# Six instead of four accumulation banks opened together at the start of each SwiGLU of a two-layer hybrid trunk

## The chip, the cores and the metric

The kernel runs on one core of a Trainium2 chip. The metric is the time of one execution on the device in microseconds (us). Three runs of the kernel before were timed, and their median stands for it. One execution was recorded by the hardware profiler, and every row below comes from that one.

Five engines matter here. PE is the matrix engine (its weight loads are shown apart, as PEld), DVE the vector engine, ACT the scalar engine, POOL the general one, and SP issues the transfers from memory. Each engine works through its own queue in order and waits on semaphores for the others.

## The reference, cut to what matters

256 tokens of width 1024 go through two layers. Each layer is a half-step SwiGLU, a mixer (neighbourhood attention beside a long convolution), a second half-step SwiGLU, and a gated per-layer input:

```python
for i in range(DEPTH):
    x = x + 0.5 * swiglu(rmsnorm(x, g_ffa[i]), w_ffa_gate[i], w_ffa_up[i], w_ffa_down[i])
    ...                                   # mixer: x = x + y @ w_out[i]
    x = x + 0.5 * swiglu(rmsnorm(x, g_ffb[i]), w_ffb_gate[i], w_ffb_up[i], w_ffb_down[i])
    x = x + jax.nn.sigmoid(rmsnorm(x, g_ple[i]) @ w_ple_gate[i]) * (p[i] @ w_ple_proj[i])
return rmsnorm(x, g_final)

def swiglu(h, w_gate, w_up, w_down):
    return (jax.nn.silu(h @ w_gate) * (h @ w_up)) @ w_down
```

So there are four SwiGLUs. The inner width is 2816, that is 22 blocks of 128 columns for the gate and 22 for the up product.

## The kernel before, in words

**Layout.** The activations are kept transposed: `x[c]`, c = 0 to 7, is a block of 128 channels by 256 tokens. For a product the block is scaled by the norm's gain and split into two parts, high and low, that lie side by side in one `xg` tile of 128x512: ACT writes the high half (L368), DVE the low half (L370), both in `prep`. The norm's factor 1/rms is not applied to the input. It is found meanwhile (`Rstd`) and multiplied onto the products later (`rb`, L444, used at L489 and L490).

**Weights.** They come as 128x128 tiles in exactly the order in which PE will use them, packed by `_weights` on the host. SP loads 16 tiles at a time (1 MB). Each half of 8 tiles is cast by ACT to a high part `wh` (L285) and DVE (at times POOL) computes the low part `wl` (L288). There are six buffers each for `wh` and `wl` (`WBUFS`), so a cast for a later half waits until PE has used up an earlier one.

**Products.** `Wide.mm` issues one wide matmul (L191: `wh` against high and low of `xg`, 512 columns) and keeps a narrow one (L200: `wl` against the high part, 256 columns) for later. After every eight wides, or when a bank's last block is reached, the kept narrow ones are issued. A gate or up block of 128 columns takes eight wides and eight narrow ones, one of each for every input block c, summed in one of the eight accumulation banks (`psp`, `bufs=8`, each 128x512). When a bank is complete, `taken` frees it: ACT copies its right half to a `gu` tile (L205) and DVE adds the left half (L208).

**The start of a SwiGLU** (`ffn`, L508 to L522). The first four banks (gate and up of the first two column blocks) are filled together: the outer loop runs over the input blocks c, the inner one over the four banks. So PE needs block c only after 4c wides. After that each further bank is filled alone, with all eight input blocks in a row (`product2`). The second loop (`DOWN`) multiplies by the down weights.

**What stands before it.** In the two SwiGLUs that follow the mixer, the eight blocks of the second half of the output projection (`project`, one bank for each block) are multiplied on DVE by the other norm's factor (L944, which reads the bank and thereby frees it), added to `x[c]` (L945), and then scaled and split (L368, L370). In the SwiGLU that follows the gated input, `update` reads the bank at L1043. The very first SwiGLU starts from the loaded input (L1090, L1093), and all banks are free.

**Order.** The side work is written as generators ("fibers"). Every three matmul steps of the main line (`TICK`) all live fibers move one step, the newest first. On PE and ACT the instructions keep this order as written. On the other engines a scheduler puts them in order when the program is built, and it hands out a bank when an older one has been freed. `onward` starts the fiber that turns a finished block into the next `xg` block.

Of the kernel before, what the change touches and what calls it, by code (L numbers as in the profile page):

```python
# [18 lines left out]
P = 128  # L19
# [3 lines left out]
KD = D // P  # L23
DFF = 2816
NF = DFF // P
NH = 8
HY = 512
EPS = 1e-6
HALF = 8
GROUP = 8  # L30

E = mybir.EngineType
# [48 lines left out]
def hybrid_trunk(ctx: ExitStack, tc: tile.TileContext, w, xT, pT, rpb, small, wf, zT, dft, idft, decay, out):  # L81
# [17 lines left out]
    def nm(s):  # L99
        uid[0] += 1  # L100
        return f"{s}{uid[0]}"

    def bank():
        return psp.tile([P, 512], F32, tag="ps", name=nm("ps"))

    def t2(dt=F32, s="t"):
        return k2.tile([P, 512], dt, tag="k2", name=nm(s))

    def t1(dt=F32, s="s"):
        return k1.tile([P, T], dt, tag="k1", name=nm(s))  # L110
# [4 lines left out]
    def f(ap):  # L115
        return ap.bitcast(F32)
# [31 lines left out]
    def spawn(gen, first=False):  # L148
        fb = Fiber(gen)
        Pace.live.insert(0 if first else len(Pace.live), fb)  # L150
        return fb
# [13 lines left out]
    def rest(n):  # L165
        for _ in range(n):
            yield
# [15 lines left out]
    class Wide:  # L183
# [6 lines left out]
        def mm(cls, b, lh, ll, r, start, stop):  # L190
            PE.matmul(b, lh, r, start=start, stop=False)  # L191
            cls.later.append((b[:, T:], ll, r[:, :T], stop))
            if stop or len(cls.later) == GROUP:
                cls.flush()
# [8 lines left out]
    def summed(dst, b):  # L203

        S.copy(dst, b[:, T:])  # L205
        yield
        yield
        V.tensor_add(dst, dst, b[:, :T])  # L208
# [39 lines left out]
    def load():  # L248
# [10 lines left out]
        elif n == 1:  # L259
            for q in range(2):  # L260
                nc.sync.dma_start(x[4 + 2 * q], xT[4 + 2 * q])
                nc.sync.dma_start(raw[:, q * HALF : (q + 1) * HALF], src[:, q * HALF : (q + 1) * HALF])
                nc.sync.dma_start(x[5 + 2 * q], xT[5 + 2 * q])
# [5 lines left out]
    def part(steps=1):  # L269
# [5 lines left out]
        raw = Stream.raws[n // 2]  # L275
        h = whp.tile([P, HALF, P], F32R, tag="wh", name=nm("wh"))
        l = wlp.tile([P, HALF, P], F32R, tag="wl", name=nm("wl"))
        fb = Fiber(None)
        Stream.ready[n] = (h, l, fb)

        def go():
            k = HALF // steps
            for a in range(0, HALF, k):
                src = raw[:, n % 2 * HALF + a : n % 2 * HALF + a + k]
                S.copy(h[:, a : a + k], src)  # L285
                yield
                e = G if Stream.on_pool and n % Stream.on_pool == 0 else V
                e.tensor_sub(l[:, a : a + k], src, f(h[:, a : a + k]))  # L288
            if n % 2:
                Stream.raws.pop(n // 2)  # L290
                load()
# [71 lines left out]
    def new_norm(join=True):  # L363
        Norm.sq = Squares(acc, KD, join)
# [8 lines left out]
    def onward(i, cg, c, before):  # L373

        hl = t2(F32R, "xg")

        def go():
            yield from before
            yield
            yield from prep(i, cg, c, hl)  # L380

        scaled.append((hl, spawn(go())))
# [68 lines left out]
    def norm(xs, at, spread=SPREAD_AT):  # L451
        return Rstd(rb, Norm.sq.parts, D, [fb for _, fb in xs.xs] + early, at, spread)
# [10 lines left out]
    def product2(b, ws, xs):  # L463
        for c in range(KD):
            wh, wl = ws.next()
            Wide.mm(b, wh, wl, xs.both(c), c == 0, c == KD - 1)


    def ffn(i, cg_next, i_next):
        act = []  # L470
        xs = Inputs()
        ws = Tiles()
        rs = norm(xs, STAT_F, SPREAD_F)

        def taken(b):
            dst = t1(s="gu")

            def go():
                yield from rest(EV)
                yield from summed(dst, b)  # L480

            return dst, spawn(go())

        def gated(gate, up, hl):
            (g, gf), (u, uf) = gate, up
            while not (gf.done and uf.done):
                yield
            yield from rs.wait()
            V.tensor_mul(g, g, rb)  # L489
            G.tensor_mul(u, u, rb)  # L490
            yield
            yield
            s = t1()
            S.activation(s, g, AF.Silu)
            yield
            yield
            V.tensor_mul(s, s, u)
            yield
            yield
            S.copy(hl[:, :T], s)  # L500
            yield
            V.tensor_sub(hl[:, T:], s, f(hl[:, :T]))

        def start(gate, up):
            hl = t2(F32R, "act")
            act.append((hl, spawn(gated(gate, up, hl))))

        heads = [bank() for _ in range(4)]  # L508
        for c in range(KD):
            for b in heads:  # L510
                wh, wl = ws.next()
                Wide.mm(b, wh, wl, xs.both(c), c == 0, c == KD - 1)
        heads = [taken(b) for b in heads]
        start(*heads[:2])
        start(*heads[2:])
        for ff in range(2, NF):
            pair = []
            for _ in range(2):
                b = bank()
                product2(b, ws, xs)  # L520
                pair.append(taken(b))
            start(*pair)  # L522
        ws = Tiles()
        new_norm()

        def half_step(c, ps):
            yield from rest(EV)
            for b in (ps[:, :T], ps[:, T:]):
                V.scalar_tensor_tensor(x[c], b, 0.5, x[c], op0=ALU.mult, op1=ALU.add)  # L529

        out = {}
        for c, k in DOWN:
            if k == 0:
                out[c] = bank()
            wh, wl = ws.next()
            hl, fb = act[k]
            fb.finish()
            Wide.mm(out[c], wh, wl, hl, k == 0, k == NF - 1)
            if k == NF - 1:
                onward(i_next, cg_next, c, half_step(c, out.pop(c)))  # L540
# [564 lines left out]
    for i in range(DEPTH):  # L1105
        Stream.on_pool = 0
        flt = spawn(filter_steps(i))
        ffn(i, C_MIX, i)
        flt.finish()
        Stream.on_pool = ON_POOL  # L1110
        mixer(i)
        Stream.on_pool = 0
        given = ple_input(i)
        ffn(i, C_PLE, i)
        ends, outs = ple(i, i == DEPTH - 1, given)
# [47 lines left out]
def _tiles(wm):  # L1163

    k, m = wm.shape
    return wm.reshape(k // P, P, m // P, P).transpose(2, 0, 1, 3)


def _weights(a):
    out = np.empty((DEPTH * PIECES * 16, P, P), np.float32)  # L1170
    at = 0

    def put(t):
        nonlocal at
        t = t.reshape(-1, P, P)
        out[at : at + len(t)] = t
        at += len(t)

    def swiglu(i, s):
        g, u = _tiles(a[f"w_ff{s}_gate"][i]), _tiles(a[f"w_ff{s}_up"][i])  # L1180
        gu = np.stack([g, u], axis=1)
        put(gu[:2].reshape(4, KD, P, P).transpose(1, 0, 2, 3))
        put(gu[2:])
        put(_tiles(a[f"w_ff{s}_down"][i])[tuple(np.array(DOWN).T)])

    for i in range(DEPTH):
        swiglu(i, "a")
        win = _tiles(a["w_in"][i])
        put(win[8:12].transpose(1, 0, 2, 3))
        for kind, j in MIXER:  # L1190
            if kind in "gqx":
                for k in {"g": (20 + j, 16 + j), "q": (j, 4 + j), "x": (12 + 2 * j, 13 + 2 * j)}[kind]:
                    put(win[k])
        wo = _tiles(a["w_out"][i])
        put(wo[:, :4])
        put(wo[:, 4:])
        swiglu(i, "b")
        put(_tiles(a["w_ple_proj"][i]))
        put(_tiles(a["w_ple_gate"][i]))
    assert at == len(out)  # L1200
    return np.ascontiguousarray(out.reshape(-1, 16, P, P).transpose(0, 2, 1, 3)).reshape(-1, P, 16 * P)
# [60 lines left out]
```

## Time and profile before

| | |
|---|---|
| median of 3 runs | 1102.88 us (1100.53 to 1103.08) |
| the profiled execution | 1100.78 us |
| its span, first to last instruction | 1099.0 us |
| PE busy | 1069.0 us, 97% of the span |
| DVE, ACT, POOL busy | 81%, 59%, 28% |
| mean granted TensorE clock | 0.994 |

The span is read against the time of the same execution: 1.78 us lie outside it. A row of a timeline gives the start and the length of a group of instructions of one engine, the line, the operation, the tiles and the count, and in brackets the idle time before it with what ended it. The length of a matmul row runs to the end of its last result, so rows overlap the next ones a little, and the pace is read from start to start. In the four SwiGLUs of this trace the first matmul on an input block stands at 6.2 us, 331.5 us, 550.0 us and 868.2 us.

### The profile page before, as it was taken

How to read it: one execution, taken by the hardware profiler on the slowest of the kernel's cores; microseconds unless marked ns; L12 is line 12 of the kernel's file. 1: busy time of each engine (PE TensorE's matmuls, PEld its weight loads, DVE VectorE, ACT ScalarE, POOL GpSimd, SP SyncE). 2: the span in 40 equal slices, each digit the busy share in tenths (PEclk: the TensorE clock that was granted, in tenths of full speed). 3: DMA queues.
4: the chain of work that ended last, by engine and by line, in shares of the span. 5: the costliest groups of instructions: out<-in, count | busy, mean ns of one | idle time of the engine just before them, and what ended most of it. 6: DMA issues, size and time to landing. Idle time of an engine off the chain costs nothing.

```text
span 1099.0 us, 17994 instructions
## 1 busy us (share of the span) xinstructions
PE 1069.0 (97%) x6716; PEld 964.8 (88%) x6716; DVE 895.5 (81%) x1552; ACT 645.6 (59%) x1182; POOL 306.8 (28%) x270
## 2 busy tenths in 40 slices
PE   7989999999998999999999999999999999999995
PEld 6878888899997888888988888889989888888895
DVE  4999987797999977766789989777899998776665
ACT  6566565377746755544656665544856575554444
POOL 3123231534363311111112113135442721111101
PEclk9999999999999999999999999999999999999998
DMA  8556554554425655555465654554522465555521
GB/s 318 196 201 230 194 189 155 185 185 154 148 78 201 199 189 190 189 192 191 155 208 185 233 192 166 186 185 152 194 77 95 147 207 215 191 193 181 185 94 38
DMA packets 32983, 194.06 MB, mean 177 GB/s; under 512 B 3584, under 2 KB 6528, under 8 KB 10880
## 3 DMA queue, kind: packets, MB, share of 16 engines
q1 hardware_dynamic: 32896, 192.92, 51.1%
q8 instruction: 52, 0.85, 0.3%
q14 instruction: 35, 0.29, 0.1%
HBM read 191.86 MB, written 1.05 MB: 176 GB/s over the span
## 4 chain that ended last, share of the span: by engine, by line
PE 80%; DVE 11%; ACT 4%; issue 3%; DMA 1%; POOL 0%; SPq 0%; DVEq 0%; ACTq 0%; POOLq 0%
PE ps L191 43%; PE ps L200 23%; PE ps L171 4%; PE ps L172 4%; PE ps L170 4%; DVE wl L288 2%; ACT wh L285 1%; DVE rt L399 1%; DVE s L841 1%; DVE x L945 1%; DVE s L944 1%; ACT t L781 1%; DMA t<-in_idft 1%; DVE xg L370 0%; DMA raw<-in_w 0%
## 5 line engine op out<-in xcount | busy, mean ns | idle before, releaser
L288 DVE TENSOR_TENSOR wl<-raw,wh 128x1024 fp32r<-128x1024 f32 (+1 forms) x328 | 416.3, 1272 | 135.1 <-ACT wh L285 113.3
L285 ACT CAST wh<-raw 128x1024 fp32r<-128x1024 f32 (+1 forms) x350 | 362.9, 1042 | 206.0 <-PE ps L191 143.5
L191 PE MATMUL ps<-xg,wh 128*128 128x512 f32 x1408 | 363.2, 396 | 12.3 <-DVE xg L1093 6.6
L191 PEld LDWEIGHTS ps<-xg,wh 128*128 128x128 f32 x1408 | 254.6, 191 | 59.4 <-DVE xg L370 7.5
L200 PEld LDWEIGHTS ps<-xg,wl 128*128 128x128 f32 x1408 | 195.4, 193 | 14.1
L200 PE MATMUL ps<-xg,wl 128*128 128x256 f32 x1408 | 200.5, 284 | 0.0
L490 POOL TENSOR_TENSOR gu<-gu,rb 128x256 f32<-128x256 f32 x88 | 94.8, 1082 | 368.1 <-DVE gu L208 288.0
L191 PE MATMUL ps<-act,wh 128*128 128x512 f32 x704 | 179.0, 392 | 0.0
L356 POOL TENSOR_TENSOR acc<-acc,q 128x256 f32<-128x256 f32 x62 | 68.9, 1112 | 283.7 <-ACT q L353 282.5
L191 PEld LDWEIGHTS ps<-act,wh 128*128 128x128 f32 x704 | 126.3, 189 | 22.1
L170 PE MATMUL ps<-xg,wh 128*128 128x256 f32 x448 | 127.5, 285 | 0.0
L172 PE MATMUL ps<-xg,wl 128*128 128x256 f32 x448 | 126.7, 283 | 0.0
L171 PE MATMUL ps<-xg,wh 128*128 128x256 f32 x448 | 126.7, 283 | 0.0
L200 PEld LDWEIGHTS ps<-act,wl 128*128 128x128 f32 x704 | 97.1, 190 | 7.6
L200 PE MATMUL ps<-act,wl 128*128 128x256 f32 x704 | 99.4, 282 | 0.0
L171 PEld LDWEIGHTS ps<-xg,wh 128*128 128x128 f32 x448 | 85.9, 192 | 0.1
L170 PEld LDWEIGHTS ps<-xg,wh 128*128 128x128 f32 x448 | 85.9, 192 | 0.1
L172 PEld LDWEIGHTS ps<-xg,wl 128*128 128x128 f32 x448 | 85.9, 192 | 0.0
L288 POOL TENSOR_TENSOR wl<-raw,wh 128x1024 fp32r<-128x1024 f32 x22 | 55.9, 2540 | 63.7 <-ACT wh L285 50.9
L208 DVE TENSOR_TENSOR gu<-gu,ps 128x256 f32<-128x256 f32 x176 | 71.9, 412 | 0.1
L205 ACT COPY gu<-ps 128x256 f32<-128x256 f32 x176 | 63.6, 369 | 0.0
L368 ACT ACTIVATE xg<-x,sm 128x256 fp32r<-128x256 f32 x56 | 28.1, 507 | 59.5 <-DVE x L529 40.2
(196 smaller groups left out, 1369.5 us busy)
## 6 DMA issues: line engine op xcount, KB each, us to landing
raw<-in_w SPq DMA_DIRECT2D x172, 1024.0 KB, 4.9
bias<-in_rpb SPq DMA_DIRECT2D x16, 256.0 KB, 2.8
raw<-in_w SPq DMA_DIRECT2D x4, 256.0 KB, 4.8
x<-in_xT SPq DMA_DIRECT2D x8, 128.0 KB, 4.7
raw<-in_w SPq DMA_DIRECT2D x2, 512.0 KB, 5.8
t<-in_wf SPq DMA_DIRECT2D x4, 256.0 KB, 5.4
dec<-in_decay SPq DMA_DIRECT2D x4, 256.0 KB, 5.4
out<-o SPq DMA_DIRECT2D x4, 256.0 KB, 2.4
```

What stands on the lines that cost most here:

```text
L170: PE.matmul(o, lh, rh, start=start, stop=False)
L171: PE.matmul(o, lh, rl, start=False, stop=False)
L172: PE.matmul(o, ll, rh, start=False, stop=stop)
L191: PE.matmul(b, lh, r, start=start, stop=False)
L200: PE.matmul(o, ll, rh, start=False, stop=stop)
L205: S.copy(dst, b[:, T:])
L208: V.tensor_add(dst, dst, b[:, :T])
L285: S.copy(h[:, a : a + k], src)
L288: e.tensor_sub(l[:, a : a + k], src, f(h[:, a : a + k]))
L356: G.tensor_add(self.ac, self.ac, q)
L368: S.activation(hl[:, :T], x[c], AF.Copy, scale=g)
L490: G.tensor_mul(u, u, rb)
```

## The change

The constant `HEADS = 3` is new, and three pairs of banks (six banks) instead of two pairs are filled in the loop over the input blocks. The host packs the weight tiles in the new order. The numbers of matmuls, casts, copies and transfers stay what they were.

```diff
+HEADS = 3
...
-        heads = [bank() for _ in range(4)]
+        heads = [bank() for _ in range(2 * HEADS)]
         for c in range(KD):
             for b in heads:
                 wh, wl = ws.next()
                 Wide.mm(b, wh, wl, xs.both(c), c == 0, c == KD - 1)
         heads = [taken(b) for b in heads]
-        start(*heads[:2])
-        start(*heads[2:])
-        for ff in range(2, NF):
+        for j in range(HEADS):
+            start(*heads[2 * j : 2 * j + 2])
+        for ff in range(HEADS, NF):
...
         gu = np.stack([g, u], axis=1)
-        put(gu[:2].reshape(4, KD, P, P).transpose(1, 0, 2, 3))
-        put(gu[2:])
+        put(gu[:HEADS].reshape(2 * HEADS, KD, P, P).transpose(1, 0, 2, 3))
+        put(gu[HEADS:])
```

## Rows read from the trace of the kernel before

**Rows 1.** PE's waits over the whole span: us in total, times, longest us.

```profile
PE ps L191 <- DVE xg L1093: 6.6, 2, 6.2
PE ps L191 <- DVE xg L370: 5.7, 5, 1.9
```

**Rows 2.** Timeline of PE, start of the SwiGLU after the first mixer.

```profile
331.52 2.12 PE L191 MATMUL ps<-xg,wh 128*128 128x512 f32 x8 [0.94 <-DVE xg L370]
...
340.24 1.75 PE L191 MATMUL ps<-xg,wh 128*128 128x512 f32 x4 [1.92 <-DVE xg L370]
...
347.72 0.50 PE L418 MATMUL ps<-onesf,acc 128*128 128x1 f32 x4
348.08 0.96 PE L191 MATMUL ps<-xg,wh 128*128 128x512 f32 x3
...
349.83 2.00 PE L191 MATMUL ps<-xg,wh 128*128 128x512 f32 x8
351.67 1.12 PE L200 MATMUL ps<-xg,wl 128*128 128x256 f32 x8
352.62 2.00 PE L191 MATMUL ps<-xg,wh 128*128 128x512 f32 x8
```

**Rows 3.** Timeline of PE, start of the SwiGLU after the second mixer.

```profile
868.18 2.12 PE L191 MATMUL ps<-xg,wh 128*128 128x512 f32 x8 [1.48 <-DVE xg L370]
...
875.24 2.14 PE L191 MATMUL ps<-xg,wh 128*128 128x512 f32 x8 [1.19 <-DVE xg L370]
...
887.46 2.00 PE L191 MATMUL ps<-xg,wh 128*128 128x512 f32 x8
```

**Rows 4.** Timeline of PE, start of the third SwiGLU, after the gated input.

```profile
549.97 2.00 PE L191 MATMUL ps<-xg,wh 128*128 128x512 f32 x8
...
567.35 2.00 PE L191 MATMUL ps<-xg,wh 128*128 128x512 f32 x8
```

**Rows 5.** Timeline of PE, start of the first SwiGLU; its four banks end at 20.98.

```profile
6.20 2.08 PE L191 MATMUL ps<-xg,wh 128*128 128x512 f32 x4 [6.20 <-DVE xg L1093]
8.65 2.07 PE L191 MATMUL ps<-xg,wh 128*128 128x512 f32 x4 [0.38 <-DVE xg L1093]
...
20.98 2.00 PE L191 MATMUL ps<-xg,wh 128*128 128x512 f32 x8
```

**Rows 6.** Stretches: us, PE busy (count), granted clock, DMA share, GB/s.

```profile
341.00:344.00 3.00, 3.00 (x13) 0.50 0.29 63
...
866.00:868.00 2.00, 0.70 (x6) 1.00 0.88 373
```

**Rows 7.** Timeline of DVE, reads that free projection banks: first two, fifth, sixth.

```profile
326.38 0.74 DVE L944 TENSOR_TENSOR s<-ps,rhy 128x256 f32<-128x256 f32 x2
...
332.52 0.41 DVE L944 TENSOR_TENSOR s<-ps,rhy 128x256 f32<-128x256 f32 x1
...
334.69 0.41 DVE L944 TENSOR_TENSOR s<-ps,rhy 128x256 f32<-128x256 f32 x1
```

**Rows 8.** The same reads after the second mixer, the fifth and the sixth.

```profile
870.07 0.41 DVE L944 TENSOR_TENSOR s<-ps,rhy 128x256 f32<-128x256 f32 x1
...
871.83 0.74 DVE L944 TENSOR_TENSOR s<-ps,rhy 128x256 f32<-128x256 f32 x2
```

**Rows 9.** Timeline of DVE, the sixth read that frees a bank of the gated input.

```profile
547.83 0.41 DVE L1043 TENSOR_TENSOR s<-ps,rb 128x256 f32<-128x256 f32 x1
```

**Rows 10.** Timelines of ACT and DVE after the first mixer: a cast, the blocks behind it.

```profile
335.12 1.03 ACT L285 CAST wh<-raw 128x1024 fp32r<-128x1024 f32 x1
...
336.42 0.51 ACT L368 ACTIVATE xg<-x,sm 128x256 fp32r<-128x256 f32 x1
...
339.71 0.47 DVE L370 SCALAR_TENSOR_TENSOR xg<-x,sm,xg 128x256 fp32r<-128x256 f32 x1
```

**Rows 11.** Timeline of DVE: the first adds that free completed gate and up banks.

```profile
31.25 1.41 DVE L208 TENSOR_TENSOR gu<-gu,ps 128x256 f32<-128x256 f32 x4
...
885.05 0.40 DVE L208 TENSOR_TENSOR gu<-gu,ps 128x256 f32<-128x256 f32 x1
```

## The prediction

> **What bounds the kernel now.** I read the busy times first: PE works 97% of the span, so only PE's pauses and the stretches at a lower clock can be won. Next I read PE's waits [rows 1]. The wides that wait for an input block are the largest entry: 6.6 us in the first SwiGLU and 5.7 us in the later ones. That is all this change can reach, and 6.2 us of the first entry is the wait for the very first block, which stays. Then I read PE's timeline at each of the four starts, to see which block is late, and DVE's timeline beside it, to see why. Last come the stretches with the granted clock.
>
> What the reader should see: after each mixer PE waits twice. It waits for the first blocks (0.94 and 1.48 us), which is unchanged, and again in the middle, for block 5 after the first mixer (1.92 us) and for block 4 after the second (1.19 us) [rows 2, 3]. After the longer middle wait the granted clock shows 0.50 for 3 us, the 1.2 GHz level, which costs 1.5 us more; after the others it stays at 1.00 [rows 6]. The third SwiGLU starts with no wait [rows 4].
>
> **What each start loses now.** A bank filled alone takes 352.62 - 349.83 = 2.79 us; eight wides take 351.67 - 349.83 = 1.84 us of it, 0.23 us each, and the eight narrow ones the other 0.95 us [rows 2]. Six banks therefore need 6 x 2.79 = 16.76 us without loss. To compare like with like I take the time from the first wide to the first wide of the seventh bank, in both kernels six full banks plus the four small statistics matmuls (348.08 - 347.72 = 0.36 us [rows 2]).
> - After the first mixer: 352.62 - 331.52 - 0.36 - 16.76 = 3.98 us lost [rows 2].
> - After the second: 887.46 - 868.18 - 0.36 - 16.76 = 2.16 us lost [rows 3].
> - Third SwiGLU: 567.35 - 549.97 - 0.36 - 16.76 = 0.26 us lost [rows 4].
> - First SwiGLU: block 1 is late by 0.38 us, and PE is slow there anyway (four wides in about 2.08 us) [rows 5].
>
> **What the change does to the blocks.** Block c is needed after 6c wides instead of 4c, so about 0.7 us later for each c. Block 5 after the first mixer is split at 339.71 + 0.47 = 340.18 us [rows 10]; with six banks it is needed after 30 wides and 24 narrow ones, 331.52 + 30 x 0.23 + 24 x 0.12 = 341.3 us at the earliest. The middle waits for blocks go. That is what the change gives.
>
> **What it adds: a wait for banks.** There are eight banks. When a SwiGLU starts after a mixer, the eight products of the projection hold up to all of them, and each comes free when DVE has read it at L944, one step ahead of the update of that very block. Four heads need four of them read, six heads need six. This is a count, so it holds for whatever order banks are handed out in. Not shown before is how long PE waits for a bank; its bounds are nothing (the reads come earlier) and the DVE rows as they stand. I take those rows, because these reads depend only on the projection and the norm, and DVE's queue ahead of them does not depend on the new loop.
> - After the first mixer the fifth and the sixth read end at 332.93 and 335.10 us [rows 7]. PE's sixth wide would be due at 331.52 + 5 x 0.23 = 332.67. It waits until 335.10: 2.43 us lost.
> - After the second the reads end at 870.48 and about 872.24 [rows 8]. The sixth wide would be due at 869.33: 2.91 us lost.
> - After the gated input the sixth read ends at 548.24 [rows 9], before the start at 549.97 [rows 4]. Nothing is lost, and the 0.26 us go.
> - In the first SwiGLU all banks are free. The wides for the two new banks fill the time from 6.20 + 4 x 0.43 = 7.9 us to 8.65 us [rows 5]: 0.75 us at half pace, worth 0.4 us.
>
> **What queues behind the new wait.** On PE everything, as it works in order. On ACT the cast at 335.12 needs the weight buffer that the first eight wides use up; those would now end near 336.0 instead of 333.4, so the cast slips by 0.9 us. Behind it on ACT stands the high half of block 5 (336.42), then near 337.4, and its low half on DVE runs at 339.71 [rows 10], so 2 us of cover remain. Block 5 is then not needed before 335.10 + 25 x 0.23 + 24 x 0.12 = 343.7 us.
>
> **What I cost at nothing.** Counts of matmuls, casts, copies and transfers do not change. SP's transfers keep their order, since PE takes the tiles one after another as packed. The generators move by matmul steps, and the number of steps before each is unchanged up to the end of the heads, so the statistics and rb keep their places in the sequence. The six evacuations (0.41 us each on DVE [rows 11]) now fall together behind the 48th wide. Their cover is the two banks left, 2 x 2.79 = 5.58 us; without that cover they are the slower rival below.
>
> **The clock.** A pause of 1.92 us was followed by 3 us at half clock [rows 2, 6]; pauses of 1.48 and 1.19 us were not [rows 3, 6]. With six heads PE does five wides between the last projection matmul and 335.10, with pauses of about 0.9, 0.5 and 1.9 us, and after the second mixer again five wides, with pauses of about 1.5, 1.1 and 1.5 us. Between no fall (0) and one like the one seen (3 x 0.5 = 1.5 us) I take the fall at both places, since the idle time there is closer to that before the fall seen than to that of the pauses without one. The Trainium skill, TensorE: Matmul & The Clock Gate, section "A second HAM failure mode: psum-queue depth-cycling", describes a kernel that paused between groups as it cycled through banks, and whose clock fell and rose again for it; by that the sum holds both falls, by the rows of the second mixer alone it holds none.
>
> **The sum.**
> - First SwiGLU: -0.4.
> - After the first mixer: 2.43 + 1.5 - 3.98 = -0.05, nothing.
> - Third SwiGLU: -0.26.
> - After the second mixer: 2.91 + 1.5 - 2.16 = +2.25.
>
> Together +1.55 us on the profiled execution's 1100.78, so 1102.3 us. That execution lies 2.1 us below the median of the runs, and on the median of 1102.88 it is 1104.4 us. About 0.3% (3.3 us) is what a measurement of this kernel can tell from no change, so this counts as the same.
>
> **The rivals.**
> - *Waits without falls.* The clock stays up at both places: -0.4 + (2.43 - 3.98) - 0.26 + (2.91 - 2.16) = -1.45 us, 1101.4 us. For it: the second mixer's pauses passed without a fall. Against: there are now three close together. Still the same within the bound.
> - *The change does all it says (faster).* DVE frees the banks in time, and all that the starts lose goes: 0.4 + 3.98 + 0.26 + 2.16 = 6.8 us, 1096.1 us. It decides where the sixth read comes before 332.67 and 869.33. Against: the rows put it 2.4 and 2.9 us later. For: DVE's order is made anew by the scheduler and could put those reads ahead of other work.
> - *The evacuation comes late (slower).* Six banks end together, and PE has two left. If the first of the six is freed more than 5.58 us after they end, the ninth bank waits. In the first SwiGLU the four heads ended at 20.98 [rows 5] and the first was freed at 31.25 + 0.41 = 31.66 [rows 11], 10.7 us later; the same delay now would cost 5.1 us, and with the rest of the sum 1109.5 us. Against: after the second mixer four heads ended near 887.46 - 2 x 2.79 - 0.36 = 881.5 and the first was freed at 885.45 [rows 3, 11], 4.0 us later, and if the adds of the first SwiGLU stay where they are, 31.66 is 5.5 us behind the new end near 26.2, just in time. The Trainium skill, Perfetto Trace Analysis, section Matmuls, asks that matmul groups rotate through banks so that the evacuation of one overlaps the matmuls of the next, which speaks for this rival; no row before shows PE waiting for it.
>
> **How the numbers follow.** Forecast (waits with a fall at one or both places) 0.60, waits without falls 0.14, all freed in time 0.11, late evacuation 0.15. The predicted time is the forecast's, 1104.4 us. The range leaves out the fast rival and the far half of the slow one (0.19 together): from the case without falls, 1101.4, less the 2.35 us by which the lowest run lies under the median, 1099.0, up to 1104.4 plus half of the late evacuation, about 1107. Chances: faster than 1099.6 is the fast rival, 0.11; slower than 1106.2 is the slow one and a little of the forecast, 0.16; the same 0.73.
>
> **What would show it.** Right: the middle waits for input blocks are gone, and right behind each mixer PE's sixth wide waits for DVE's L944, with starts near 335.1 and 872.2; the granted clock is low behind them; the third SwiGLU starts without a wait. Wrong: no such waits (then the fast rival), or PE waits near the ninth bank for L208 (then the slow one), or the rows of DVE before the sixth read stand in another order.

## The result and the profile after

The changed kernel takes 1102.18 us (median of 22 runs, 1100.13 to 1106.8), the kernel before, in the 22 runs taken beside it, 1100.41 us (1098.62 to 1103.22). The ratio is 1.0021 with a 95% interval of 1.0011 to 1.003: +1.2 to +3.3 us. That is a loss small enough to count as the same by the bound of 0.3%, and it has the sign and about the size of the forecast: 1102.18 - 1100.41 = +1.77 us against +1.55 us.

The profiled execution of the changed kernel is the longest of its 22 runs: 1106.8 us, with a span of 1105.0 us. What follows shows where the time goes; its total is more than a typical run loses. Behind the line of the new constant, line numbers are one higher than before: L192, L201, L371, L945, L209, L419 are what were L191, L200, L370, L944, L208, L418. So L945 is from here on the read that frees a projection bank.

First the page's engine shares and the row of the granted clock in 40 slices:

```profile
span 1105.0 us, 17990 instructions
...
PE 1074.6 (97%) x6716; PEld 970.2 (88%) x6716; DVE 897.5 (81%) x1552; ACT 647.0 (59%) x1182; POOL 308.8 (28%) x270
...
PEclk9999999999998999999999999999999899999998
```

PE has the same share as before. Besides the last slice, two of the clock stand out, the 13th (from 331.5 us, behind the first mixer) and the 32nd (from 856.4 us, behind the second).

PE's waits over the whole span (us in total, times, longest us) answer to [rows 1]:

```profile
PE ps L192 <- DVE xg L1094: 7.1, 1, 7.1
PE ps L192 <- DVE s L945: 4.3, 4, 1.6
...
PE ps L192 <- DVE xg L371: 2.4, 2, 1.5
```

The waits for input blocks fell from 5.7 us in five to 2.4 us in two, the two for the first blocks behind the mixers. In their place stands an entry that was not there: 4.3 us in four waits for DVE's L945, the instruction that reads the projection's banks. PE's wait for the very first block grew from 6.2 to 7.1 us because the first transfers landed later in this execution: ACT's first cast of weights, which waits for them, begins at 5.33 us, where it began at 4.41.

The timeline of PE behind the first mixer answers to [rows 2]:

```profile
330.58 1.20 PE L192 MATMUL ps<-xg,wh 128*128 128x512 f32 x4 [0.94 <-DVE xg L371]
332.06 0.50 PE L192 MATMUL ps<-xg,wh 128*128 128x512 f32 x1 [0.27 <-DVE s L945]
334.18 1.65 PE L192 MATMUL ps<-xg,wh 128*128 128x512 f32 x3 [1.62 <-DVE s L945]
...
337.34 3.34 PE L192 MATMUL ps<-xg,wh 128*128 128x512 f32 x8
...
353.12 2.00 PE L192 MATMUL ps<-xg,wh 128*128 128x512 f32 x8
```

Four wides go into free banks. The fifth waits 0.27 us and the sixth 1.62 us for a bank. From 334.18 the matmuls are at half pace (eight wides take 3.34 us instead of 2.00), and the seventh bank begins at 353.12. In between, no wait for a block is left. Behind the second mixer the same picture answers to [rows 3]:

```profile
869.72 1.21 PE L192 MATMUL ps<-xg,wh 128*128 128x512 f32 x4 [1.48 <-DVE xg L371]
872.06 0.49 PE L192 MATMUL ps<-xg,wh 128*128 128x512 f32 x1 [1.13 <-DVE s L945]
873.79 1.65 PE L192 MATMUL ps<-xg,wh 128*128 128x512 f32 x3 [1.23 <-DVE s L945]
...
892.56 2.00 PE L192 MATMUL ps<-xg,wh 128*128 128x512 f32 x8
```

The reads on DVE that free those banks, the fifth and the sixth of each projection, answer to [rows 7, 8]:

```profile
331.59 0.41 DVE L945 TENSOR_TENSOR s<-ps,rhy 128x256 f32<-128x256 f32 x1
...
333.71 0.41 DVE L945 TENSOR_TENSOR s<-ps,rhy 128x256 f32<-128x256 f32 x1
...
871.60 0.41 DVE L945 TENSOR_TENSOR s<-ps,rhy 128x256 f32<-128x256 f32 x1
...
873.32 0.74 DVE L945 TENSOR_TENSOR s<-ps,rhy 128x256 f32<-128x256 f32 x2
```

Each ends just ahead of the wide that waited: 331.59 + 0.41 = 332.00 for the wide at 332.06, 334.12 for 334.18. PE follows DVE here, read for read.

The granted clock (us, PE busy and matmuls, clock, DMA share, GB/s) answers to [rows 6]:

```profile
334.20:337.00 2.80, 2.80 (x10) 0.50 0.89 357
337.00:341.00 4.00, 4.00 (x16) 0.60 0.00 0
815.00:825.00 10.00, 8.65 (x54) 0.83 0.01 2
873.00:876.00 3.00, 2.21 (x7) 0.50 0.88 354
876.00:879.00 3.00, 3.00 (x11) 0.50 0.00 1
879.00:881.00 2.00, 2.00 (x13) 0.87 0.16 20
```

Behind both waits the clock is at its lower level, 1.2 GHz, for some 6 us of PE's work. The stretch from 815 to 825 us lies inside the second mixer, which the change does not touch; there the clock was 1.00 before. The last section comes back to it.

**Where the 6.0 us of the two profiled executions lie** (1106.8 - 1100.78), from the same milestones in both traces:

| Stretch | Before | After | Difference |
|---|---|---|---|
| to the 7th bank of the first SwiGLU | 26.57 | 26.44 | -0.13 |
| on to the first wide behind mixer 1 | 304.95 | 304.14 | -0.81 |
| start behind mixer 1, to the 7th bank | 21.10 | 22.54 | +1.44 |
| on to the third SwiGLU | 197.35 | 197.35 | 0.00 |
| its start, to the 7th bank | 17.38 | 17.22 | -0.16 |
| on to the first wide behind mixer 2 | 300.83 | 302.03 | +1.20 |
| start behind mixer 2, to the 7th bank | 19.28 | 22.84 | +3.56 |
| the rest | 213.32 | 214.24 | +0.92 |

The four starts together are +4.7 us of it. The other +1.3 us lie in stretches whose instructions are the same, but for the evacuation of the six banks behind the first row; the fall of the clock at 815 us belongs to them.

### The profile page after: what moved, and what is told of

Its sections match the earlier page's. It is cut to its first block, busy times and chain, and to the rows that moved or that the text cites. A ratio compares the mean times of both kernels' runs of the same rounds, so it can differ in the third digit from the quotient of the medians.

```text
span 1105.0 us, 17990 instructions
## 1 busy us (share of the span) xinstructions
PE 1074.6 (97%) x6716; PEld 970.2 (88%) x6716; DVE 897.5 (81%) x1552; ACT 647.0 (59%) x1182; POOL 308.8 (28%) x270
## 3 DMA queue, kind: packets, MB, share of 16 engines
HBM read 191.86 MB, written 1.05 MB: 175 GB/s over the span
## 4 chain that ended last, share of the span: by engine, by line
PE 77%; DVE 12%; ACT 4%; issue 3%; DMA 2%; POOL 1%; SPq 0%; DVEq 0%; ACTq 0%; POOLq 0%
PE ps L192 42%; PE ps L201 22%; PE ps L172 4%; PE ps L173 4%; PE ps L171 4%; DVE wl L289 3%; DMA raw<-in_w 2%; ACT wh L286 2%; DVE rt L400 1%; DVE s L842 1%; ACT t L782 1%; DVE s L945 1%; DMA t<-in_idft 1%; ACT t L775 0%; DVE y L811 0%
## 5 line engine op out<-in xcount | busy, mean ns | idle before, releaser
L192 PE MATMUL ps<-xg,wh 128*128 128x512 f32 x1408 | 366.7, 398 | 13.9 <-DVE xg L1094 7.1
L192 PEld LDWEIGHTS ps<-xg,wh 128*128 128x128 f32 x1408 | 256.8, 192 | 61.3 <-DVE xg L1094 7.1
L201 PEld LDWEIGHTS ps<-xg,wl 128*128 128x128 f32 x1408 | 196.8, 193 | 14.3
L201 PE MATMUL ps<-xg,wl 128*128 128x256 f32 x1408 | 202.6, 285 | 0.0
L192 PE MATMUL ps<-act,wh 128*128 128x512 f32 x704 | 179.0, 392 | 0.0
L192 PEld LDWEIGHTS ps<-act,wh 128*128 128x128 f32 x704 | 126.2, 189 | 22.1
L201 PEld LDWEIGHTS ps<-act,wl 128*128 128x128 f32 x704 | 97.1, 190 | 7.6
L201 PE MATMUL ps<-act,wl 128*128 128x256 f32 x704 | 99.4, 282 | 0.0
L209 DVE TENSOR_TENSOR gu<-gu,ps 128x256 f32<-128x256 f32 x176 | 70.9, 412 | 0.1
```

Source lines behind the costliest of these rows:

```text
L201: PE.matmul(o, ll, rh, start=False, stop=stop)
```

## The experiments

The theory: what decides is the wait for projection banks behind the two mixers, with the fall of the clock that follows it. Rivals: the loss comes from somewhere else in the new loop, also where no mixer stands ahead (the six banks that end together); or it is a matter of which block arrives when. Each kernel below was timed in five rounds. The kernel before took 1100.55 us beside the first four (22 runs) and 1100.22 us beside the last three (17 runs). All compute the whole reference. The edits shift the line numbers. The wide matmul is L196 in the first two kernels, L192 in the two that start from the changed kernel, and L200, L201 and L200 in the three with the third pair late; the tiles and the counts of a row tell which it is. The start of a SwiGLU "loses" what the prediction means by it: its time to the seventh bank less 16.76 us and, where the statistics' matmuls lie inside it, 0.36 us.

### Six banks only where no mixer stands ahead, and only behind the mixers

The first kernel keeps six banks in the first and the third SwiGLU and goes back to four behind the mixers; the second does the opposite.

```diff
-HEADS = 3
+def plan(s):
+    pairs = 3 if s == "a" else 2      # the second kernel: 2 and 3
+    return pairs, [(c, j) for c in range(8) for j in range(2 * pairs)]
...
+        s = "a" if cg_next == C_MIX else "b"
+        pairs, seq = plan(s)
...
+        for c, j in seq:
+            wh, wl = ws.next()
+            Wide.mm(heads[j], wh, wl, xs.both(c), c == 0, c == KD - 1)
```

> Edit: six heads only in the two SwiGLUs that no mixer stands before (the first and the third); four heads, as before, in the two that follow a mixer. My theory (what the change loses, it loses to the wait for the projection's banks and to the lower clock behind it, only after a mixer): both L945-type waits of PE are gone, the granted clock behind the mixers is as in the kernel before, and the time is 0.1 to 0.6 us under the kernel before (ratio about 0.9997). Rival (the loss comes from six banks that end together, or from the new order of the weights, wherever six are used): half of the loss stays, about +0.9 us, ratio 1.0008.

Measured: 1099.42 us (1097.3 to 1101.1, 11 runs), ratio 0.9988 (0.9978 to 0.9998), -1.1 us, where 0.1 to 0.6 us less had been expected. PE has no wait for a read of a projection bank. So the half of the change that stands behind no mixer is a small gain, and the rival that put the loss there, at 1.0008, is out.

> Edit: the other half: six heads only in the two SwiGLUs that follow a mixer, four in the first and the third. My theory: all of the loss is here; PE's fifth and sixth wide wait for DVE's L945 (1.6 to 2.4 us in each of the two places), the clock falls behind at least one of them, and the time is 1.8 to 3 us over the kernel before (ratio 1.0015 to 1.003), no better than the change itself. Rival (late evacuation anywhere): about +0.9 us, ratio 1.0008.

Measured: 1104.55 us (1102.79 to 1107.85, 6 runs), ratio 1.0048 (1.0034 to 1.0061), +4.0 us. This half holds the whole loss. It is more than was expected; the two halves together give -1.1 + 4.0 = +2.9 us, inside the +1.2 to +3.3 us of the whole change. It waits 4.0 us in four for the banks. Its PE behind the first mixer, and its clock there and behind the second:

```profile
329.76 1.20 PE L196 MATMUL ps<-xg,wh 128*128 128x512 f32 x4 [0.95 <-DVE xg L375]
331.23 0.49 PE L196 MATMUL ps<-xg,wh 128*128 128x512 f32 x1 [0.27 <-DVE s L950]
333.36 0.96 PE L196 MATMUL ps<-xg,wh 128*128 128x512 f32 x3 [1.64 <-DVE s L950]
...
349.56 2.00 PE L196 MATMUL ps<-xg,wh 128*128 128x512 f32 x8
```

```profile
334.00:337.00 3.00, 3.00 (x19) 1.00 0.58 227
...
870.00:873.00 3.00, 3.00 (x13) 0.50 0.35 131
873.00:876.00 3.00, 3.00 (x15) 0.78 0.00 0
```

The waits behind the first mixer have the lengths that they have in the changed kernel (0.27 and 1.64 us), and yet the clock stayed at 1.00. Three wides take 0.96 us here and 1.65 us there. That start loses 349.56 - 329.76 - 0.36 - 16.76 = 2.68 us, 1.3 us less than before. Behind the second mixer the clock fell and the start lost 5.42 us. So the wait for banks comes in both traces, and the fall behind it does not.

### The banks copied out on ACT

The changed kernel, with the projection's banks read by a copy on ACT that waits for the product alone; DVE then works from the copy.

```diff
-                yield from add(c, ps, hy, V)
+                yield from rest(EV)
+                t = t1()
+                S.copy(t, ps)
+                yield from hy.wait()
+                V.tensor_mul(t, t, hy.dst)
+                V.tensor_add(x[c], x[c], t)
```

> Edit: six heads everywhere, and the eight projection banks before a SwiGLU are copied out by ACT one step after each is complete, so that they come free without waiting for the norm and for DVE; DVE then multiplies the copy. Eight ACT copies of about 0.36 us are added for each mixer. My theory: no wait of PE for a bank is left, the blocks are in time, and what the two starts lost before goes (3.98 and 2.16 us), together with the small gains of the other two: 1094 to 1096 us beside 1100.4, ratio 0.994 to 0.996. Rival (the wait for banks only stood in front of another wait, for the blocks that the same DVE queue delivers): the two starts still lose 2 us or more each, the time stays within 2 us of the kernel before, ratio 0.998 to 1.002.

Measured: 1107.53 us (1104.87 to 1110.01, 6 runs), ratio 1.0066 (1.0051 to 1.008). A miss, with the wrong sign. PE's wait over the span and ACT's rows ahead of the first mixer's end say why:

```profile
PE ps L192 <- ACT s L1003: 7.9, 4, 3.7
```

```profile
326.47 0.91 ACT L369 ACTIVATE xg<-x,sm 128x256 fp32r<-128x256 f32 x2 [3.69 <-DVE x L1006]
...
333.68 0.36 ACT L1003 COPY s<-ps 128x256 f32<-128x256 f32 x1
```

ACT works in the order written. The copies stand behind scalings of input blocks that wait for DVE (3.69 us idle), so the banks come free later than in the changed kernel, and behind the first mixer PE's sixth wide waits 3.67 us for its copy. The edit did not take the wait away; it moved it to the copy and made it 7.9 us long. What it shows is that PE's wait goes with whatever reads the banks. How much a truly earlier release would give was not measured by it.

### The third pair late

Behind the mixers, blocks 0 to 3 go into four banks first, then into the third pair, then blocks 4 to 7 into all six. PE asks for the fifth and sixth bank after 16 wides instead of 4, and is busy meanwhile.

```diff
+def plan(s):
+    if s == "a":
+        return 3, [(c, j) for c in range(8) for j in range(6)]
+    seq = [(c, j) for c in range(4) for j in range(4)]
+    seq += [(c, j) for c in range(4) for j in (4, 5)]
+    seq += [(c, j) for c in range(4, 8) for j in range(6)]
+    return 3, seq
...
```

> Edit: six heads everywhere, but after a mixer the third pair starts late: blocks 0 to 3 go into the first four banks, then blocks 0 to 3 into the last two, then blocks 4 to 7 into all six; the weights are packed in that order. My theory: the sixth bank is then needed only after 18 wides (about 6 us after the start), long after it is free (3.6 and 4.1 us after the start in the trace of the change), and the eight extra wides stand exactly where PE waited for blocks 4 and 5: no wait but the first is left and the clock stays up, 1094 to 1096 us, ratio 0.994 to 0.996. Rival (DVE's blocks are the limit whatever the order of the banks): waits of 1 us or more for L371 remain at blocks 4 to 7, ratio 0.998 to 1.001.

Measured: 1096.38 us (1094.79 to 1098.89, 11 runs), ratio 0.9967 (0.9957 to 0.9977), -4.2 us, a little short of the 1094 to 1096 us expected. The starts behind the mixers now lose 0.23 and 0.41 us, where the change loses 5.42 and 5.72. The wait for banks is gone, the waits in the middle for blocks are gone too, and so are both falls of the clock behind the starts. That is the main evidence for the theory: the same six banks, asked for later, are a gain. But a new wait stands among PE's (first line: us, times, longest), at the ninth bank behind either mixer and, with 0.77 us, in the first SwiGLU:

```profile
PE ps L200 <- DVE gu L217: 3.4, 3, 1.6
```

```profile
353.60 0.96 PE L200 MATMUL ps<-xg,wh 128*128 128x512 f32 x3 [1.58 <-DVE gu L217]
...
889.00 1.43 PE L200 MATMUL ps<-xg,wh 128*128 128x512 f32 x5 [1.01 <-DVE gu L217]
```

```profile
349.18 0.70 ACT L445 ACTIVATE s<-ident,rl 128x128 fp32r<-128x128 f32 x2 [6.49 <-DVE rl L440]
349.78 1.98 ACT L294 CAST wh<-raw 128x1024 fp32r<-128x1024 f32 x2
351.66 1.73 ACT L214 COPY gu<-ps 128x256 f32<-128x256 f32 x6
```

```profile
353.13 2.07 DVE L217 TENSOR_TENSOR gu<-gu,ps 128x256 f32<-128x256 f32 x6
```

The six banks end by 346.28. ACT, in its own order, first waits 6.49 us for the statistics (L445, the scaling of the identity by the norm's factor), then does two casts of weights, and only then the six copies that DVE's adds need. The first bank is free at 353.13 + 0.41 = 353.54, 7.3 us after the end. Two more banks last 5.58 us, so the ninth is late. This is the slow rival of the prediction; in the changed kernel it is hidden because PE, held up at the start, ends the six banks later: there they end 1.3 us behind the start of that scaling (353.12 against 351.83), here 2.9 us ahead of it (346.28 against 349.18).

### The wait filled with work

The changed kernel, with six more wides ahead of the fifth bank's first one behind each mixer. They write the bank that is started anew right behind them.

```diff
         for c in range(KD):
-            for b in heads:
+            for j, b in enumerate(heads):
                 wh, wl = ws.next()
+                if c == 0 and j == 4 and cg_next == C_PLE:
+                    for _ in range(6):
+                        PE.matmul(b, wh, xs.both(c), start=True, stop=True)
```

> Edit: the change as it is, but after a mixer six extra wides (block 0, a result that the bank's first real wide overwrites) are put into the fifth bank before its own first wide. They need only what that wide needs, and last 6 x 0.23 = 1.4 us, less than the 1.6 and 1.2 us for which PE waits for the sixth bank, so the waits should end when they did. My theory (the lower clock behind the waits comes from PE's idling there and is about half of the loss): the granted clock stays at 1.00 behind both mixers, the six banks after the first mixer lose about 2.4 us instead of 5.4 and after the second about 3.4 instead of 5.7 (the extra wides themselves in the place of waiting), and the time is 1.5 to 3.5 us under the change: ratio to the kernel before 0.998 to 1.000. Rival (the clock falls for another reason, or not more often than before): low clock in the same places, ratio 1.001 to 1.003.

Measured: 1099.55 us (1097.93 to 1101.99, 12 runs), ratio 0.9996 (0.9983 to 1.0008): with twelve wides more it is level with the kernel before, and under the changed kernel, whose interval begins at 1.0011. The mean granted clock of its 12 runs is 0.993, that of the changed kernel's 22 runs 0.990. PE and the clock behind the first mixer, then behind the second:

```profile
330.16 1.65 PE L515 MATMUL ps<-xg,wh 128*128 128x512 f32 x6 [0.28 <-DVE s L948]
332.30 0.96 PE L192 MATMUL ps<-xg,wh 128*128 128x512 f32 x3 [0.25 <-DVE s L948]
...
866.22 2.93 PE L515 MATMUL ps<-xg,wh 128*128 128x512 f32 x6 [1.15 <-DVE s L948]
```

```profile
330.00:334.00 4.00, 3.59 (x18) 1.00 0.80 273
...
866.00:869.00 3.00, 2.78 (x7) 0.52 0.85 309
869.00:871.00 2.00, 2.00 (x13) 0.87 0.45 163
```

Behind the first mixer the six wides fill the sixth bank's wait and the clock stays up; the start loses 348.49 - 328.69 - 17.12 = 2.68 us, as in the kernel without a fall above. Since that kernel kept its clock there without a filling, this one trace does not show that the filling kept it up; the runs together speak for it. Behind the second the pauses of 1.48 and 1.15 us come ahead of the filling, the clock falls all the same, and part of the low stretch lies under the added wides; that start loses 4.52 us instead of 5.72, where 3.4 was expected. PE has more to do and takes the banks no earlier, yet the time is some 2.5 us under the changed kernel's: part of the change's cost is thus the clock and not the wait as such.

### The third pair late, and its banks read earlier

Two ways to take the new wait out of the kernel with the late pair. In the first, the four early banks also end early, and each bank, in every SwiGLU, is handed to its evacuation as it ends:

```diff
-    seq += [(c, j) for c in range(4, 8) for j in range(6)]
+    seq += [(c, j) for c in range(4, 8) for j in range(4)]
+    seq += [(c, j) for c in range(4, 8) for j in (4, 5)]
...
             Wide.mm(heads[j], wh, wl, xs.both(c), c == 0, c == KD - 1)
+            if c == KD - 1:
+                heads[j] = taken(heads[j])
```

> Edit: the late third pair, which now also ends late: blocks 0 to 3 into four banks, then into the last two, then blocks 4 to 7 into the four, then into the two; a bank's evacuation is started when it is complete. So four banks end after 40 wides and two after 48. My theory of what the late pair still lost (PE waited 1.6 and 1.0 us for L208-type adds at the ninth bank, because six copies on ACT queue behind the norm's small matmul scale, L436 of before, and two casts): the copies of the first four now stand directly behind that scale and before the casts, the first bank is free 2 to 3 us earlier, and both waits go: 1 to 3 us under the version with the late pair, about 1094 to 1095.5, ratio 0.994 to 0.9957. Rival (the ACT queue stays blocked until the same time, or blocks 6 and 7 are late after 32 wides): a wait of 0.5 us or more in their place and no gain over the late pair, ratio 0.996 to 0.998.

Measured: 1093.26 us (1092.37 to 1094.39, 6 runs), ratio 0.9931 (0.9915 to 0.9947), -7.0 us, more than the 1094 to 1095.5 us expected. The starts lose 0.32 and 0.22 us, and no wait for an evacuation is left. Its evacuations behind the first mixer:

```profile
348.18 0.70 ACT L446 ACTIVATE s<-ident,rl 128x128 fp32r<-128x128 f32 x2 [6.48 <-DVE rl L441]
348.78 0.90 ACT L215 COPY gu<-ps 128x256 f32<-128x256 f32 x3
```

```profile
349.17 1.08 DVE L218 TENSOR_TENSOR gu<-gu,ps 128x256 f32<-128x256 f32 x3 [0.62 <-ACT gu L215]
```

ACT still waits 6.48 us for the statistics, but copies come right behind it and ahead of the casts. The first bank is free near 349.6, 4.2 us after the sixth ends at 345.38, inside the 5.58.

In the second, the order of the late pair stays as it was and the statistics go six matmul steps later behind the mixers, so that ACT meets the copies first:

```diff
-        rs = norm(xs, STAT_F, SPREAD_F)
+        rs = norm(xs, STAT_F + (6 if s == "b" else 0), SPREAD_F)
```

> Edit: the late pair with all six ending together, as in the run before it, and the norm's statistics after a mixer six steps later (18 wides), so that the six copies stand ahead of the norm's scale in ACT's queue. My theory: the same as for the late end: the copies run right after the 54th wide instead of some 5 us later, PE no longer waits for the ninth bank, 1 to 3 us under the version with the late pair, ratio 0.994 to 0.9957. Rival (the statistics come too late and the 15 small buffers for gate and up fill up, as rb comes 18 wides later): a new wait of 1 us or more for a gu buffer, ratio 0.997 or more.

Measured: 1092.82 us (1091.16 to 1093.48, 6 runs), ratio 0.9924 (0.9908 to 0.9941), -7.4 us. One wait of 0.4 us for an evacuation is left, in the first SwiGLU. ACT's rows behind the first mixer now stand in the other order:

```profile
347.53 1.73 ACT L214 COPY gu<-ps 128x256 f32<-128x256 f32 x6
...
353.40 0.69 ACT L445 ACTIVATE s<-ident,rl 128x128 fp32r<-128x128 f32 x2 [4.14 <-DVE rl L440]
```

The two cannot be told from each other (their intervals overlap). Both are faster than the change, and faster than the kernel before by about the 6.8 us that the prediction worked out for a change that does all it says. Two different edits of the kernel with the late pair, which share only an earlier read of the banks, remove the waits behind the mixers. It is thus shown that their cause was the burst of evacuations standing in ACT's order behind the statistics and the casts.

## Why the prediction was right

**What the change gives** was right. The middle waits for blocks are gone [rows 2, 3], and the third SwiGLU starts without loss (0.10 us for 0.26). The first SwiGLU needs 26.44 - 7.12 = 19.32 us from its first wide to the seventh bank, where it needed 20.37; that is 1.05 us less for the 0.4 predicted, but it began 0.92 us later, so the blocks had more time and the seventh bank gained 0.13.

**The wait for banks** was right to 0.02 us. The sixth wide was due at 330.58 + 1.15 = 331.73 and ran at 334.18, 2.45 us late (2.43 predicted). Behind the second mixer it was due at 870.87 and ran at 873.79, 2.92 us late (2.91). The reason why the old rows could be used held: DVE's order ahead of those reads did not change.

**The falls of the clock** came at both places in the profiled execution, as forecast, but their price there was mis-sized. It is what the start lost beyond its bank wait: 5.42 - 2.45 = 2.97 us and 5.72 - 2.92 = 2.80 us, where 1.5 us each had been taken from the one fall seen before [rows 6]. These two prices are the step of the prediction that was off by most: the clock stayed low for some 6 us of PE's work, not 3. Their excess makes up the 2.8 us by which the four starts (+4.7) exceed the sum of +1.55, beside 0.4 us in the first and third SwiGLU. The prediction's reading that the clock stayed up behind the second mixer's pauses goes beyond [rows 6], which end at 868 us, but it holds: the trace before has 1.00 on to 880 us. The Trainium skill, TensorE: Matmul & The Clock Gate, section "A second HAM failure mode: psum-queue depth-cycling", was cited for falls at this kind of pause; the changed kernel's trace agrees (0.50 behind both), and the run with the same 1.64 us wait at a clock of 1.00 does not.

**Why the sum still came out** at +1.77 us between the medians: with no fall behind the first mixer the starts would be at -0.13 + (2.68 - 3.98) - 0.16 + 3.56 = +2.0 us, close to that. So a fall at one place and none at the other would do. How often each fall comes cannot be counted, since one execution of each kernel has a trace, but the mean granted clock of every run is on record:

| Mean granted clock | Kernel before, 39 runs beside the experiments | Changed kernel, 22 runs |
|---|---|---|
| mean of the runs | 0.9935 | 0.9896 |
| median time of the runs at 0.992 | 1101.62 us (3 runs) | 1100.34 us (6 runs) |
| median time of the runs at 0.990 | 1102.71 us (9 runs) | 1102.21 us (3 runs) |
| times of the runs at 0.988 or less | none | 1104.01 to 1106.8 us (8 runs) |

The changed kernel's spread goes with the clock, and at the same clock it is 0.5 to 1.3 us under the kernel before, near the -1.45 us that the rival without falls gave. So what the medians lose goes with the clock. The sizes are rough, as the runs at one clock are few and the clock is given to 0.001; which falls they were, the means do not tell. Two errors of the prediction stand against each other: a fall costs nearly twice what was taken, and does not come every time. That the sum of +1.55 us lies so close to +1.77 us is in this part luck.

**The base** was off by 2.2 us. The prediction added 2.1 us since the profiled execution lay below the median of three runs; 22 runs put the median at 1100.41, and the profiled 1100.78 is a usual one. On that base the sum gives 1102.3 us, and 1102.18 was measured. The three runs shown are the first of these 22; that two of them were among the longest was chance. The 16.76 us for six banks is 6 x 2.79 = 16.74 by the rounded pace shown, which moves no loss by more than 0.02 us.

**Two smaller steps failed without cost.** The cast behind the new wait did not slip by 0.9 us. It began 3.57 us after the first wide, and 3.60 us before [rows 2, 10], so it does not need the buffer that the first eight wides use up:

```profile
334.15 1.03 ACT L286 CAST wh<-raw 128x1024 fp32r<-128x1024 f32 x1
```

And "the number of steps before each is unchanged" was not true in the first SwiGLU: L419's matmuls stand after 69 wides there, L418's stood after 54. PE was not seen to wait for what follows from them.

**The rivals.** "Late evacuation" was given 0.15 and a deciding point of 5.58 us. In the changed kernel the first of the six is free at 355.77 + 0.41 = 356.18 behind the first mixer, 3.1 us after they end:

```profile
355.77 2.07 DVE L209 TENSOR_TENSOR gu<-gu,ps 128x256 f32<-128x256 f32 x6
```

Only in the first SwiGLU does it show, with 0.28 us. There the first add begins at 31.84 us, so the first bank is free at 32.25 us, 5.81 us after the six end at 26.44 and past the 5.58: the ninth bank begins at 32.30, where the eighth's start plus a bank's 2.79 us gives 32.02.

```profile
29.23 2.00 PE L192 MATMUL ps<-xg,wh 128*128 128x512 f32 x8
...
32.30 1.42 PE L192 MATMUL ps<-xg,wh 128*128 128x512 f32 x5
```

The kernel with the late pair then showed the rival in full (3.4 us in three waits), past the point worked out for it: 7.3 us against 5.58 behind the first mixer. The rule from the Trainium skill, Perfetto Trace Analysis, section Matmuls, that groups should rotate through banks so that evacuation overlaps the next group, agrees with that run. The price of "all it says" was near what was found, though by another order of the work: the kernels without bank waits behind the mixers gain 7.0 and 7.4 us for the 6.8 worked out.

**Still open:** what decides whether the clock falls behind a pause. Also open in part is why the half behind the mixers alone costs 4.0 us in the median, more than its profiled execution (1102.79, +2.0 us on the profiled one before). That execution has the highest clock of its six runs, 0.992; the other five, at 0.986 to 0.990, take 1103.87 to 1107.85 us. But at the same clock it is still 1.7 to 2.5 us above the changed kernel, and the gain of the other half explains only 1.1 us of that.

## What to carry to other kernels

Count the buffers at the seam of two stages: where the stage ahead holds all the banks, a stage that opens n at once waits until n of them have been read. Where those reads do not depend on the new stage, they stand in the trace of the old kernel, and the wait could be read off there to 0.02 us. Open only as many as are free, keep the engine busy on them, and take the others later. Then look at the other end: banks that finish together need their evacuation at once, so whatever the evacuating engine is to do first, in its written order, must not wait for something else.

## What the runs showed of the hardware

The same wait was not always followed by the same clock. Five wides with pauses of 0.94, 0.27 and 1.62 us ahead of and among them were followed by some 6 us at 1.2 GHz (334.2 to about 340.2) in the changed kernel; pauses of 0.95, 0.27 and 1.64 us at the same place, with the same matmuls between, left the clock at 1.00 in the kernel with six banks behind the mixers only. The low stretches also lasted longer than the one of the kernel before, about 6 us against 3 us [rows 6], so one fall seen is no price for the next.

The fall from 815 to 825 us in the changed kernel is of the same kind. Inside the second mixer PE pauses once for 1.18 to 1.20 us in all nine traces. Shortly behind that pause the clock fell in four of them: the changed kernel, the one with the copies on ACT, the one with the third pair late and the one whose late pair also ends late. It stayed at 1.00 in the other five, the kernel before among them. The two with a late pair have no wait for projection banks, so the fall is not that wait's doing. The kernel before and the one with the third pair late (us, PE busy and matmuls, clock, DMA share, GB/s):

```profile
815.00:825.00 10.00, 8.64 (x68) 1.00 0.01 2
```

```profile
815.00:825.00 10.00, 9.91 (x69) 0.83 0.27 90
```
